# A two-layer hybrid block kernel: residual in a DRAM buffer during the mixers, shared half tiles, later decay tables, due dates for readers of PSUM

## The chip, the cores and the metric

The kernel runs on one core of a Trainium2 chip. The metric is the device time of one execution in microseconds (us). A core has a matrix engine (TensorE, in the profile PE, its weight loads PEld), a vector engine (VectorE, DVE), a scalar engine (ScalarE, ACT), GpSimd (POOL), and SyncE (SP), which here only issues DMA transfers. All of them work on an on-chip memory of 128 partitions (SBUF). TensorE writes to a smaller memory of eight banks (PSUM), which VectorE and ScalarE read.

## The reference

Two layers, 256 latent tokens and 256 context tokens, width 1024, all in fp32. Cut to what matters, for one stream:

```python
for l in range(DEPTH):
    mod = silu(c) @ w_mod[l] + b_mod[l]                  # 6 vectors of 1024: shift, scale, gate, twice
    h = rms_norm(x, norm_gain[l, 0]) * (1 + mod[1]) + mod[0]
    p = split_cols(h @ w_in[l])                          # q, k, v of four mixers, gate logits
    a, b, c_, d = gqa(p), retention(p), mla(p), diff_attention(p)
    y = sum(sigmoid(gate_n) * (mixer_n @ w_branch[l, n]) for n in range(4)) @ w_out[l]
    x = x + mod[2] * y
    h2 = rms_norm(x, norm_gain[l, 1]) * (1 + mod[4]) + mod[3]
    g, u = split(h2 @ w_ffn_in[l])
    x = x + mod[5] * ((silu(g) * u) @ w_ffn_out[l])      # hidden width 2816
```

The context goes through the same weights. Its queries are worked out in layer 0 only, since the second layer's context output is not needed.

## The kernel before

**Arithmetic.** Every fp32 matrix product is three products of a faster type: an operand is split into a rounded part (hi) and the remainder (lo), and hi\*hi, hi\*lo and lo\*hi are added up in a PSUM bank. For a weight unit of 128 x 512 the rounded copy (`whi`) is made by ScalarE or VectorE (`cp`) and the remainder (`wlo`) by VectorE (`tt`). The weights come in 512 KB loads (`wraw`, `mraw`) on SP's queue.

**Order.** The program is not run in the order in which it is written. `Builder` writes all operations to a `Recorder`. `schedule` first goes through them from the end (`backward`) and so gets for each operation the latest time at which it may end. `forward` then plays the engines with a cost for each operation: an engine that is free takes, among the operations whose inputs are ready, the one with the earliest due time. The orders thus found are emitted, one fixed queue for each engine. An operation that has variants (`cp`: ScalarE or VectorE) goes to the engine that is free, if `worth` says that the other would not finish sooner; `MARGIN` is added for the engine that isn't the first choice. `behind(lag)` keeps an operation from going before the TensorE operation that stands `lag` places ahead of it in the program.

**Tiles.** Nearly all data live in tiles of 128 x 512 fp32 of one common pool (`u`), of which there are `NU`; weight tiles may hold `W_LIMIT` of them. An operation whose output tile finds no free place in the pool is passed over by the planner (`allowed`). A PSUM tile is one of the eight banks.

**Stages of a layer.** The normed input is made in `gen_d` from the residual `xT` (eight tiles, fixed before the change) as eight tiles `hh` and eight `hl`. The projections of the mixers (`fill_*`) and the work of the heads (`jobs_*`: scores, softmax, transposes, products with v) are interleaved; head results go to `o`, four tiles for each mixer. Retention (`fill_ret`, `jobs_ret`) comes last and needs the decay tables (`rel`). Some gate logits are made early (`gate_logits`, tiles `glog`). Then `merge` multiplies each mixer's `o`, split by `split_o`, with its branch weights and sums the gated products (`glog`, `sig`); `out_proj` is the output projection, and only there `residual` updates `xT`. `ffn_in` and `ffn_out` follow; the split hidden values (`fh`, `fl`) are 44 tiles. In layer 0 a tile holds 512 tokens, in layer 1 only the 256 latent ones, so that half of such a tile is empty. `mod_vector` works out the vectors of `mod` ahead of their use, as sums of products on VectorE (`macc`).

Of the kernel before, what the change touches and what calls it, by code (L numbers as in the profile page):

```python
# [11 lines left out]
F32 = mybir.dt.float32  # L12
# [13 lines left out]
GRID_W = 64  # L26
OFF_GATE = 4512

NU = 73
DMA_LAT = 2.5  # L30
LOOKAHEAD = 1
RAW_BUFS = 7
# [1 line left out]
WRAW_LIMIT = 4  # L34
MRAW_LIMIT = 4
SLACK = 1
MARGIN = {"vector": -0.3, "scalar": -0.1, "gpsimd": 0}
W_LIMIT = 34
MOD_LAG = 600
REL_LAG = 200  # L40
DECAY_LAG = 0

MODS = {(0, ("merge", 1, 1)): [(0, 2, 2, 0.36)], (0, ("merge", 2, 1)): [(0, 3, 2, 0.385)],
# [20 lines left out]
class Recorder:  # L64
# [221 lines left out]
    def forward(self, users, deps, prio):  # L286
# [27 lines left out]
        self.times = {}  # L314

        held = 0.0

        def begin(v):
            return max(now, held) if v[6] else now
# [30 lines left out]
        while len(order) < n:  # L350
            while wait and wait[0][0] <= now + 1e-9:
                _, i = heapq.heappop(wait)
                for v in ops[i][0]:
                    heapq.heappush(heaps[v[0]], (prio[i], i))
            while ends and ends[0][0] <= now + 1e-9:
                _, i = heapq.heappop(ends)
                done[i] = True
                for nm in ops[i][2]:
                    t = tiles[nm]
                    t[3] -= 1  # L360
                    if t[3] == 0:
                        for tag in t[0]:
                            live[tag] -= 1
                            prof[tag][low:t[2] + 1] -= 1
                while low < n and done[low]:
                    low += 1
            nxt = wait[0][0] if wait else 1e18
            if ends:
                nxt = min(nxt, ends[0][0])
            for e in self.ENGINES:  # L370
                h = heaps[e]
                while h and issued[h[0][1]]:
                    heapq.heappop(h)
                if not h:
                    continue
                if free[e] > now + 1e-9:
                    nxt = min(nxt, free[e])
                    continue
                skipped = []
                found = -1  # L380
                while h and len(skipped) < 200:
                    p, i = heapq.heappop(h)
                    if issued[i]:
                        continue
                    if allowed(i) and (len(ops[i][0]) == 1 or worth(e, i, p)):
                        found = i
                        break
                    skipped.append((p, i))
                for x in skipped:
                    heapq.heappush(h, x)  # L390
                if found < 0:
                    continue
                i = found
                issued[i] = True
                for nm in ops[i][2]:
                    t = tiles[nm]
                    if not t[4]:
                        t[4] = True
                        for tag in t[0]:
                            live[tag] += 1  # L400
                            if t[1] > low:
                                prof[tag][low:t[1]] += 1
                pick[i] = next(x for x, v in enumerate(ops[i][0]) if v[0] == e)
                v = ops[i][0][pick[i]]
                end = begin(v) + v[4]
                free[e] = end
                if v[6]:
                    held = end
                self.times[i] = now
                if e == "sync":  # L410
                    free[e] = max(end, now + 0.565)
                heapq.heappush(ends, (end + (DMA_LAT if e == "sync" else 0.0), i))
                order.append(i)
                for u in users[i]:
                    left[u] -= 1
                    w = ops[u][0][0][0]
                    lat = 0.0 if e == "tensor" == w else v[5] + self.EXTRA[w]
                    est[u] = max(est[u], end + lat)
                    if not left[u]:
                        heapq.heappush(wait, (est[u], u))  # L420
                nxt = min(nxt, free[e])
            if nxt >= 1e18:
                raise RuntimeError("schedule stuck")
            now = max(now, nxt)
# [90 lines left out]
class Builder:  # L515
    def __init__(self, ctx, tc, a, out):
        self.tc, self.nc, self.a, self.out = tc, Recorder(tc.nc), a, out
        self.pool = ctx.enter_context(tc.tile_pool(name="sb", bufs=1))
        self.psum = ctx.enter_context(tc.tile_pool(name="ps", bufs=1, space=bass.MemoryType.PSUM))
        self.w = Weights(self)  # L520


# [119 lines left out]
    def setup(self):  # L642
# [3 lines left out]
        self.featT = self.fixed([128, 160], "featT")  # L646
        self.sil = self.fixed([128, 256], "sil")
        self.modT = [self.fixed([128, 96], "modT%d" % l) for l in range(DEPTH)]
        self.xT = [self.fixed([128, 512], "xT%d" % d) for d in range(KD)]
        nc.scalar.dma_start(out=self.ident, in_=a["ident"])  # L650
        rows0 = self.u(name="rows0")
        rows1 = self.u(name="rows1")
# [140 lines left out]
    def gen_d(self, l, which, ds):  # L793

        nc = self.nc
        nd = len(ds)
        av = self.sm(2 * nd).rearrange("p (d s) -> p d s", s=2)
        s0, s1 = min(self.rb), max(self.rb) + 1
        g = self.featT[:, 96 + 16 * l + 8 * which + ds[0]:96 + 16 * l + 8 * which + ds[0] + nd]
        c1 = 3 * which + 1  # L800
        nc.vector.scalar_tensor_tensor(
            out=av[:, :, s0:s1], in0=self.modT[l][:, 16 * c1 + 2 * ds[0]:16 * c1 + 2 * ds[0] + 2 * nd].rearrange(
                "p (d s) -> p d s", s=2)[:, :, s0:s1], scalar=1.0,
            in1=g.rearrange("p (d o) -> p d o", o=1).to_broadcast([128, nd, s1 - s0]), op0=ALU.add, op1=ALU.mult)
        for i, d in enumerate(ds):
            if d == len(self.hh):
                self.hh.append(self.u(F32R, "hhi"))
                self.hl.append(self.u(F32R, "hlo"))
            hi, lo = self.hh[d], self.hl[d]
            t = self.u(name="xn")  # L810
            for s, rb in self.rb.items():
                c = slice(s * 256, s * 256 + 256)
                nc.vector.scalar_tensor_tensor(out=t[:, c], in0=self.xT[d][:, c], scalar=av[:, i, s:s + 1],
                                               in1=rb, op0=ALU.mult, op1=ALU.mult)
                bias = self.mod(l, 3 * which, s)[:, d:d + 1]
                nc.scalar.activation(out=hi[:, c], in_=t[:, c], func=AF.Identity, bias=bias)
            for s in self.rb:
                c = slice(s * 256, s * 256 + 256)
                bias = self.mod(l, 3 * which, s)[:, d:d + 1]
                nc.vector.scalar_tensor_tensor(out=lo[:, c], in0=t[:, c], scalar=bias, in1=hi[:, c].bitcast(F32),  # L820
                                               op0=ALU.add, op1=ALU.subtract)


    def proj_tok(self, n, pairs, lhs, nk, kper, evac, cols=None):
# [464 lines left out]
    def fill_ret(self, l, qp, B):  # L1289
        nc = self.nc  # L1290
        B.update({"q": {}, "k": {}, "v": [{}, {}], "g": [{}, {}]})
        H = (self.hh, self.hl)
        self.rel = (self.u(name="rel0"), self.u(name="rel1"), self.u(name="rel2"))
        for i, n in enumerate((512, 512, 128)):
            with nc.behind(REL_LAG):
                nc.sync.dma_start(out=self.rel[i][:, :n], in_=self.a["rel"][:, 512 * i:512 * i + n])
        yield from self.heads_chunk(H, qp, 4, self.tabs["ret"], None, B["q"], None, norm=False)
        yield from self.heads_chunk(H, (0, 1), 4, self.tabs["ret"], None, B["k"], None, norm=False)
        for j in range(2):
# [356 lines left out]
    def jobs_ret(self, B, o):  # L1656
# [2 lines left out]
        qp = B["qp"]  # L1659
        qt = [t for p in qp for t in (2 * p, 2 * p + 1)]  # L1660
        st = {}
        rel0, rel1, rel2 = self.rel


        def decay(h):
# [121 lines left out]
    def gate_logits(self, tok, keep):  # L1787

        ps = [self.ps_acc(), self.ps_acc()]
        yield from self.proj_feat(2, (self.hh, self.hl), KD, tok, ps)  # L1790
        for m in range(2):
            g = self.u(name="glog")
            self.cp(g[:, :tok], ps[m][:, :tok])
            keep.append(g)

    def split_o(self, n, tok):
        hi_l, lo_l = [], []
        for k in range(4):
            hi = self.u(F32R, "ohi")
            lo = self.u(F32R, "olo")  # L1800
            self.split(hi[:, :tok], lo[:, :tok], self.o[n][k][:, :tok])
            hi_l.append(hi)
            lo_l.append(lo)
        self.o[n] = (hi_l, lo_l)
# [95 lines left out]
    def out_proj(self, l, tok, mp):  # L1900
# [4 lines left out]
        def flush():  # L1905
            for d in self.pend:
                self.stats(d, tok)
            self.pend = []
        if mp == 3 and tok == 512:
            yield from self.last_pair(l, 2, self.yy, KD, flush)  # L1910
            return
# [20 lines left out]
    def ffn_in(self, l, tok, j):  # L1932
# [29 lines left out]
        yield from self.proj_feat(2, H, KD, tok, pu)  # L1962
        for m in range(2):
            self.tt(sg[m][:, :tok], pu[m][:, :tok], sg[m][:, :tok], ALU.mult)
            hi = self.u(F32R, "fhi")
            lo = self.u(F32R, "flo")
            self.split_half(hi[:, :tok], lo[:, :tok], sg[m][:, :tok])
            self.fh.append(hi)
            self.fl.append(lo)
# [102 lines left out]
    def plan(self, l):  # L2072
# [12 lines left out]
            self.step(lst, gen, cost)  # L2085

        def newo(n):
            self.o[n] = [self.u(name="o") for _ in range(4)]
            return self.o[n]

        def start():
# [173 lines left out]
```

## Time and profile before

| | us |
|---|---|
| median of 3 runs | 1778.12 |
| lowest, highest | 1776.82, 1778.41 |
| the profiled execution | 1776.79 |
| its span, first to last instruction | 1774.9 |
| TensorE busy | 1726.4 |
| VectorE busy | 1334.3 |
| ScalarE busy | 846.9 |

Busy times are shares of one span and lie beside each other. Matmuls overlap in TensorE's pipeline and their ends are modelled, so that a busy TensorE isn't one at its peak. All recorded operations have line 432, that of the recorder's emission; they are told apart by their tiles. A row names the output tile, an arrow, and the inputs.

### The profile page before, as it was taken

What the parts mean: (1) busy time and instruction counts of PE and PEld (TensorE: products, weight loads), DVE (VectorE), ACT (ScalarE), POOL (GpSimd) and SP (SyncE); (2) the same over time, 40 slices, a digit from 0 to 9 for tenths busy, and PEclk for the clock granted to TensorE, in tenths of its full rate; (3) what the DMA queues carried; (4) which work ended last, traced back from release to release, by engine and by line L of the source; (5) the groups of instructions that cost most, each with busy time, mean ns of one, the idle gap of its engine ahead of it and who ended that gap; (6) DMA issues with size and microseconds to landing.
All of it is one profiled execution on the core that took longest, in us unless ns stands there. A gap on an engine that the chain in (4) does not pass through costs nothing. (4 is left out here: it accounts for less than half of the span.)

```text
span 1774.9 us, 30925 instructions
## 1 busy us (share of the span) xinstructions
PE 1726.4 (97%) x11510; PEld 1564.5 (88%) x11510; DVE 1334.3 (75%) x3055; ACT 846.9 (48%) x2014; POOL 58.7 (3%) x89
## 2 busy tenths in 40 slices
PE   7999999999899999999999999998999899999999
PEld 5988999998687887878888789997999789999999
DVE  5899999888989678786436533989989796786563
ACT  4378665556423333532222322666655544564441
POOL 0010000001010000000000000000000100000000
PEclk9999999999999999999999999999999999999999
DMA  9413113334546465355226522342234576756451
GB/s 310 165 45 117 50 35 110 93 96 125 166 154 193 151 214 166 108 189 189 83 72 197 189 89 75 110 118 63 72 93 129 148 222 190 233 161 183 138 187 62
DMA packets 204345, 243.72 MB, mean 137 GB/s; under 512 B 9994, under 2 KB 183204, under 8 KB 204196
## 3 DMA queue, kind: packets, MB, share of 16 engines
q1 hardware_dynamic: 203840, 241.61, 44.4%
q8 instruction: 90, 1.47, 0.3%
q14 instruction: 59, 0.48, 0.1%
q10 hardware_dynamic: 356, 0.14, 0.0%
HBM read 224.15 MB, written 1.05 MB: 127 GB/s over the span
## 5 line engine op out<-in xcount | busy, mean ns | idle before, releaser
L432 ACT CAST whi<-wraw 128x512 fp32r<-128x512 f32 (+3 forms) x630 | 361.1, 605 | 353.6 <-PE ps_acc L432 160.3
L432 DVE TENSOR_TENSOR wlo<-wraw,whi 128x512 fp32r<-128x512 f32 (+4 forms) x674 | 436.4, 668 | 120.2 <-PE ps_acc L432 65.7
L432 PE MATMUL ps_acc<-hhi,wlo 128*128 128x256 f32 (+1 forms) x864 | 292.7, 339 | 8.9 <-DVE wlo L432 6.1
L432 PE MATMUL ps_acc<-hlo,whi 128*128 128x256 f32 (+1 forms) x864 | 289.7, 335 | 0.2
L432 PE MATMUL ps_acc<-hhi,whi 128*128 128x256 f32 (+1 forms) x864 | 289.4, 335 | 0.0
L432 PE MATMUL ps_acc<-whi,hhi 128*128 128x256 f32 (+2 forms) x896 | 262.5, 293 | 1.2 <-ACT x L432 0.9
L432 PE MATMUL ps_acc<-wlo,hhi 128*128 128x256 f32 (+2 forms) x896 | 254.5, 284 | 0.3 <-DVE wlo L432 0.3
L432 PE MATMUL ps_acc<-whi,hlo 128*128 128x256 f32 (+2 forms) x896 | 254.6, 284 | 0.0
L432 PEld LDWEIGHTS ps_acc<-hhi,wlo 128*128 128x128 f32 x864 | 164.6, 191 | 28.4 <-DVE wlo L432 7.7
L432 PEld LDWEIGHTS ps_acc<-hlo,whi 128*128 128x128 f32 x864 | 164.6, 190 | 17.3 <-DVE hlo L432 0.7
L432 PEld LDWEIGHTS ps_acc<-hhi,whi 128*128 128x128 f32 x864 | 164.7, 191 | 14.9
L432 PEld LDWEIGHTS ps_acc<-whi,hhi 128*128 128x128 f32 x896 | 171.2, 191 | 3.0 <-ACT x L432 1.3
L432 PEld LDWEIGHTS ps_acc<-wlo,hhi 128*128 128x128 f32 x896 | 171.4, 191 | 1.0 <-DVE wlo L432 0.5
L432 PEld LDWEIGHTS ps_acc<-whi,hlo 128*128 128x128 f32 x896 | 171.0, 191 | 0.0
L432 DVE SCALAR_TENSOR_TENSOR macc<-mraw,sil,macc 128x512 f32<-128x512 f32 x224 | 157.8, 752 | 15.7 <-DMA mraw<-in_w_mod_dram 13.4
L432 PE MATMUL ps_acc<-fhi,wlo 128*128 128x256 f32 (+1 forms) x396 | 127.5, 322 | 0.0
L432 PE MATMUL ps_acc<-flo,whi 128*128 128x256 f32 (+1 forms) x396 | 126.2, 319 | 0.0
L432 PE MATMUL ps_acc<-fhi,whi 128*128 128x256 f32 (+1 forms) x396 | 126.1, 319 | 0.0
L432 PE MATMUL ps_s<-hhi,wlo 128*128 128x512 f32 (+1 forms) x352 | 119.2, 339 | 1.3 <-ACT hhi L432 1.3
L432 PE MATMUL ps_s<-hlo,whi 128*128 128x512 f32 (+1 forms) x352 | 119.1, 338 | 0.5 <-DVE hlo L432 0.5
L432 PE MATMUL ps_s<-hhi,whi 128*128 128x512 f32 (+1 forms) x352 | 119.0, 338 | 0.0
L432 PE MATMUL ps_s<-ohi,wlo 128*128 128x512 f32 (+1 forms) x256 | 88.4, 345 | 6.7 <-DVE glog L432 6.6
(247 smaller groups left out, 3563.5 us busy)
## 6 DMA issues: line engine op xcount, KB each, us to landing
wraw<-in_w_in_dram SPq DMA_DIRECT2D x124, 512.0 KB, 4.6
mraw<-in_w_mod_dram SPq DMA_DIRECT2D x96, 512.0 KB, 4.8
wraw<-in_w_ffn_in_dram SPq DMA_DIRECT2D x88, 512.0 KB, 3.5
wraw<-in_w_ffn_out_dram SPq DMA_DIRECT2D x40, 512.0 KB, 4.6
wraw<-in_w_branch_dram SPq DMA_DIRECT2D x32, 512.0 KB, 3.6
wraw<-in_w_out_dram SPq DMA_DIRECT2D x16, 512.0 KB, 4.9
stb<-sthi SPq DMA_DIRECT2D x36, 128.0 KB, 2.3
std<-stlo SPq DMA_DIRECT2D x24, 128.0 KB, 2.3
```

The costliest lines, as they stand in the source:

```text
L432: getattr(getattr(self.nc, eng), m)(*a, **k)
```

## The change

- `xT` moves from fixed tiles into the pool, and the pool grows by the eight tiles that this frees (`NU` 73 to 81). After the normed input for the mixers is made, `store` writes `xT` to a DRAM buffer `away`; in layer 1 only the latent half. `fetch`, at the start of each `out_proj`, loads the two tiles that it updates into new tiles of the pool, at the earliest some 60 places ahead in the program (`FETCH_LAG`).
- In layer 1 two half-filled tiles become one: gate logits, the split of `o`, the split hidden values, and `o` itself.
- The decay tables are loaded when the head work of retention is written, at most 100 places ahead (`REL_LAG` 200 before), and not when its projections are.
- When an operation that reads or writes PSUM on another engine than TensorE becomes ready, its due time is set to at most 12 us (`DUE`) after that moment.
- `MARGIN` for VectorE goes from -0.3 to 0.3; `W_LIMIT` from 34 to 40.

```diff
--- before.py
+++ after.py
@@ -26,7 +26,7 @@
 GRID_W = 64
 OFF_GATE = 4512
 
-NU = 73
+NU = 81
 DMA_LAT = 2.5
 LOOKAHEAD = 1
 RAW_BUFS = 7
@@ -34,10 +34,12 @@
 WRAW_LIMIT = 4
 MRAW_LIMIT = 4
 SLACK = 1
-MARGIN = {"vector": -0.3, "scalar": -0.1, "gpsimd": 0}
-W_LIMIT = 34
+DUE = 12.0
+MARGIN = {"vector": 0.3, "scalar": -0.1, "gpsimd": 0}
+W_LIMIT = 40
 MOD_LAG = 600
-REL_LAG = 200
+REL_LAG = 100
+FETCH_LAG = 60
 DECAY_LAG = 0
 
 MODS = {(0, ("merge", 1, 1)): [(0, 2, 2, 0.36)], (0, ("merge", 2, 1)): [(0, 3, 2, 0.385)],
@@ -314,6 +316,9 @@
         self.times = {}
 
         held = 0.0
+        prio = list(prio)
+        horizon = -min(prio)
+        reader = [o[0][0][0] != "tensor" and any(x.startswith("ps_") for x in o[2]) for o in ops]
 
         def begin(v):
             return max(now, held) if v[6] else now
@@ -350,6 +355,8 @@
         while len(order) < n:
             while wait and wait[0][0] <= now + 1e-9:
                 _, i = heapq.heappop(wait)
+                if reader[i]:
+                    prio[i] = min(prio[i], est[i] - horizon + DUE)
                 for v in ops[i][0]:
                     heapq.heappush(heaps[v[0]], (prio[i], i))
             while ends and ends[0][0] <= now + 1e-9:
@@ -517,6 +524,7 @@
         self.tc, self.nc, self.a, self.out = tc, Recorder(tc.nc), a, out
         self.pool = ctx.enter_context(tc.tile_pool(name="sb", bufs=1))
         self.psum = ctx.enter_context(tc.tile_pool(name="ps", bufs=1, space=bass.MemoryType.PSUM))
+        self.dram = ctx.enter_context(tc.tile_pool(name="dr", bufs=1, space=bass.MemoryType.DRAM))
         self.w = Weights(self)
 
 
@@ -646,7 +654,8 @@
         self.featT = self.fixed([128, 160], "featT")
         self.sil = self.fixed([128, 256], "sil")
         self.modT = [self.fixed([128, 96], "modT%d" % l) for l in range(DEPTH)]
-        self.xT = [self.fixed([128, 512], "xT%d" % d) for d in range(KD)]
+        self.xT = [self.u(name="xT") for d in range(KD)]
+        self.away = [self.tile(self.dram, [128, 512], F32, "away%d" % d, "away%d" % d, 1) for d in range(KD)]
         nc.scalar.dma_start(out=self.ident, in_=a["ident"])
         rows0 = self.u(name="rows0")
         rows1 = self.u(name="rows1")
@@ -819,6 +828,23 @@
                 bias = self.mod(l, 3 * which, s)[:, d:d + 1]
                 nc.vector.scalar_tensor_tensor(out=lo[:, c], in0=t[:, c], scalar=bias, in1=hi[:, c].bitcast(F32),
                                                op0=ALU.add, op1=ALU.subtract)
+            if which == 0:
+                self.store(l, d)
+
+    def store(self, l, d):
+
+        lo, hi = 256 * min(self.rb), 256 * max(self.rb) + 256
+        if l == DEPTH - 1:
+            hi = min(hi, 256)
+        if lo < hi:
+            self.nc.sync.dma_start(out=self.away[d][:, lo:hi], in_=self.xT[d][:, lo:hi])
+
+    def fetch(self, tok, ds):
+
+        for d in ds:
+            self.xT[d] = self.u(name="xT")
+            with self.nc.behind(FETCH_LAG):
+                self.nc.sync.dma_start(out=self.xT[d][:, :tok], in_=self.away[d][:, :tok])
 
 
     def proj_tok(self, n, pairs, lhs, nk, kper, evac, cols=None):
@@ -1290,10 +1316,6 @@
         nc = self.nc
         B.update({"q": {}, "k": {}, "v": [{}, {}], "g": [{}, {}]})
         H = (self.hh, self.hl)
-        self.rel = (self.u(name="rel0"), self.u(name="rel1"), self.u(name="rel2"))
-        for i, n in enumerate((512, 512, 128)):
-            with nc.behind(REL_LAG):
-                nc.sync.dma_start(out=self.rel[i][:, :n], in_=self.a["rel"][:, 512 * i:512 * i + n])
         yield from self.heads_chunk(H, qp, 4, self.tabs["ret"], None, B["q"], None, norm=False)
         yield from self.heads_chunk(H, (0, 1), 4, self.tabs["ret"], None, B["k"], None, norm=False)
         for j in range(2):
@@ -1659,7 +1681,11 @@
         qp = B["qp"]
         qt = [t for p in qp for t in (2 * p, 2 * p + 1)]
         st = {}
-        rel0, rel1, rel2 = self.rel
+        rel = (self.u(name="rel0"), self.u(name="rel1"), self.u(name="rel2"))
+        for i, n in enumerate((512, 512, 128)):
+            with nc.behind(REL_LAG):
+                nc.sync.dma_start(out=rel[i][:, :n], in_=self.a["rel"][:, 512 * i:512 * i + n])
+        rel0, rel1, rel2 = rel
 
 
         def decay(h):
@@ -1788,16 +1814,23 @@
 
         ps = [self.ps_acc(), self.ps_acc()]
         yield from self.proj_feat(2, (self.hh, self.hl), KD, tok, ps)
+        g = self.u(name="glog")
         for m in range(2):
-            g = self.u(name="glog")
-            self.cp(g[:, :tok], ps[m][:, :tok])
-            keep.append(g)
+            if m and tok == 512:
+                g = self.u(name="glog")
+            gv = g[:, m * 256:m * 256 + 256] if tok == 256 else g
+            self.cp(gv, ps[m][:, :tok])
+            keep.append(gv)
+
+    def parts(self, tok, name):
+
+        hi = self.u(F32R, name + "hi")
+        return (hi[:, 0:256], hi[:, 256:512]) if tok == 256 else (hi, self.u(F32R, name + "lo"))
 
     def split_o(self, n, tok):
         hi_l, lo_l = [], []
         for k in range(4):
-            hi = self.u(F32R, "ohi")
-            lo = self.u(F32R, "olo")
+            hi, lo = self.parts(tok, "o")
             self.split(hi[:, :tok], lo[:, :tok], self.o[n][k][:, :tok])
             hi_l.append(hi)
             lo_l.append(lo)
@@ -1906,6 +1939,7 @@
             for d in self.pend:
                 self.stats(d, tok)
             self.pend = []
+        self.fetch(tok, (2 * mp, 2 * mp + 1))
         if mp == 3 and tok == 512:
             yield from self.last_pair(l, 2, self.yy, KD, flush)
             return
@@ -1962,8 +1996,7 @@
         yield from self.proj_feat(2, H, KD, tok, pu)
         for m in range(2):
             self.tt(sg[m][:, :tok], pu[m][:, :tok], sg[m][:, :tok], ALU.mult)
-            hi = self.u(F32R, "fhi")
-            lo = self.u(F32R, "flo")
+            hi, lo = self.parts(tok, "f")
             self.split_half(hi[:, :tok], lo[:, :tok], sg[m][:, :tok])
             self.fh.append(hi)
             self.fl.append(lo)
@@ -2085,7 +2118,10 @@
             self.step(lst, gen, cost)
 
         def newo(n):
-            self.o[n] = [self.u(name="o") for _ in range(4)]
+            if last:
+                self.o[n] = [t[:, c:c + 256] for t in [self.u(name="o") for _ in range(2)] for c in (0, 256)]
+            else:
+                self.o[n] = [self.u(name="o") for _ in range(4)]
             return self.o[n]
 
         def start():
```

## Rows read from the trace of the kernel before

**Rows 1.** The page's first part: busy time, share of the span, instructions.
```profile
PE 1726.4 (97%) x11510; PEld 1564.5 (88%) x11510; DVE 1334.3 (75%) x3055; ACT 846.9 (48%) x2014; POOL 58.7 (3%) x89
```

**Rows 2.** By stage: us; busy (count) of PE, PEld, DVE, ACT, POOL; PEclk, DMA share, GB/s.
```profile
0.00:70.00 70.00, 60.24 (x485) 48.57 (x486) 47.66 (x163) 34.51 (x80) 0.52 (x5) 1.00 0.90 301
...
70.00:425.00 355.00, 351.33 (x2693) 335.03 (x2692) 322.65 (x837) 228.75 (x597) 20.61 (x36) 1.00 0.28 80
...
425.00:450.00 25.00, 22.67 (x136) 19.59 (x135) 23.79 (x70) 17.21 (x48) 3.02 (x4) 1.00 0.23 63
...
475.00:500.00 25.00, 19.68 (x80) 15.78 (x79) 22.85 (x35) 5.46 (x9) 4.03 (x3) 0.86 0.49 149
...
500.00:725.00 225.00, 225.00 (x1037) 182.80 (x1036) 175.20 (x289) 71.91 (x136) 11.81 (x11) 1.00 0.57 180
...
1200.00:1230.00 30.00, 22.81 (x144) 18.85 (x143) 28.69 (x80) 18.72 (x45) 2.45 (x2) 0.94 0.07 19
...
1385.00:1450.00 65.00, 54.46 (x386) 51.21 (x385) 56.65 (x156) 31.55 (x76) 4.01 (x6) 0.92 0.61 183
...
1450.00:1570.00 120.00, 119.35 (x991) 118.11 (x991) 88.52 (x181) 64.43 (x145) 0.00 (x0) 1.00 0.71 217
```

**Rows 3.** The same view of two dense stretches and one without transfers.
```profile
800.00:850.00 50.00, 50.00 (x222) 41.41 (x221) 27.40 (x43) 13.27 (x23) 0.00 (x0) 1.00 0.54 176
...
1600.00:1650.00 50.00, 50.00 (x419) 50.00 (x418) 30.56 (x62) 23.88 (x51) 0.00 (x0) 1.00 0.59 180
...
70.00:80.00 10.00, 10.00 (x84) 10.00 (x83) 7.78 (x25) 2.39 (x6) 0.00 (x0) 1.00 0.00 1
```

**Rows 4.** Timeline at 479: start, us, engine, operation, xcount [idle before <-releaser].
```profile
478.85 5.39 DVE L432 SCALAR_TENSOR_TENSOR macc<-mraw,sil,macc 128x512 f32<-128x512 f32 x8
...
484.15 1.28 DVE L432 SCALAR_TENSOR_TENSOR glog<-glog,ps_s 128x512 f32<-128x512 f32 x2
...
484.89 0.79 PE L432 MATMUL ps_s<-ohi,wlo 128*128 128x512 f32 x1 [5.32 <-DVE glog L432]
```

**Rows 5.** Timeline at 1216, ScalarE, VectorE and TensorE.
```profile
1217.82 0.64 ACT L432 COPY pvl<-ps_v 64x256 f32<-64x256 f32 x2 [2.68 <-DVE mq L432]
...
1218.50 0.42 DVE L432 TENSOR_TENSOR o<-ps_v,pvl 64x256 f32<-64x256 f32 x1
...
1218.97 0.58 PE L432 MATMUL ps_v<-pthi,v 128*128 128x256 f32 x1 [2.68 <-DVE o L432]
```

**Rows 6.** Timeline from 1385, VectorE.
```profile
1385.20 0.43 DVE L432 CAST whi<-wraw 128x512 fp32r<-128x512 f32 x1 [0.66 <-PE ps_acc L432]
...
1386.52 0.69 DVE L432 TENSOR_TENSOR wlo<-wraw,whi 128x512 fp32r<-128x512 f32 x1 [0.89 <-PE ps_acc L432]
```

**Rows 7.** Waits of TensorE in 1385 to 1450: us in total, times, longest.
```profile
PE ps_acc L432 <- DVE wlo L432: 5.5, 3, 2.5
...
PE ps_v L432 <- DVE ptlo L432: 1.8, 4, 0.5
...
PE ps_v L432 <- DVE pthi L432: 1.2, 2, 0.6
```

**Rows 8.** Groups by line, whole span, copies: xcount | busy us, mean ns | idle before.
```profile
L432 DVE CAST pthi<-ps_t 128x512 fp32r<-128x512 f32 x33 | 22.5, 684 | 2.8 <-PE ps_t L432 2.6
...
L432 DVE CAST whi<-wraw 128x512 fp32r<-128x512 f32 (+2 forms) x44 | 16.9, 385 | 9.7 <-DMA wraw<-in_w_in_dram 6.2 <-PE ps_acc L432 3.5
...
L432 ACT CAST pthi<-ps_t 128x512 fp32r<-128x512 f32 x67 | 38.5, 586 | 17.2 <-PE ps_t L432 13.1 <-PE ps_v L432 3.1 <-DVE o L432 0.4
...
L432 ACT CAST whi<-wraw 128x512 fp32r<-128x512 f32 (+3 forms) x630 | 361.1, 605 | 353.6 <-PE ps_acc L432 160.3 <-PE ps_s L432 56.3 <-DMA wraw<-in_w_in_dram 43.2
```

**Rows 9.** Waits of SP's queue in the opening, 0 to 62.
```profile
SPq L432 <- PE ps_acc L432: 15.2, 9, 3.7
```

**Rows 10.** DMA issues: xcount, KB each, median us to landing.
```profile
rel<-in_rel_dram SPq DMA_DIRECT2D x4, 256.0 KB, 2.7
...
out_dram<-out SPq DMA_DIRECT2D x4, 256.0 KB, 2.5
```

## The prediction

> **What bounds the kernel now.** I read the page's first part first [rows 1]: TensorE is busy 1726.4 of 1774.9 us, VectorE 75%, ScalarE 48%. So TensorE is the bound nearly everywhere, its instructions are not changed by the diff, and all there is to win is the time in which it stands still or runs at the lower clock. Then the table by stage [rows 2] says where that is. TensorE is idle 9.8 us in the opening (0 to 70), 3.7 in the whole of 70 to 425, 2.3 in 425 to 450, 5.3 in 475 to 500, 7.2 in 1200 to 1230 and 10.5 in 1385 to 1450; 500 to 725 has none. Idle time is not all that is lost, because matmuls overlap in the pipeline and their ends are modelled. A dense stretch gives the pace [rows 3]: 222 matmuls in 50 us where they are 512 columns wide (0.225 us each), 419 where they are 256 wide (0.119 us each). By that pace the 80 wide ones of 475 to 500 need 18.0 us, so 7.0 are lost there; the 386 of 1385 to 1450 need 46 us, so up to 19 are lost; the 144 of 1200 to 1230 need 17.2, so up to 12.8 (some are 512 wide, so less). The clock column gives the part that is not idle: it falls to 0.86, 0.92 and 0.94 in just these stretches.
>
> Next, what TensorE waits for in them. At 479 it wants a PSUM bank that VectorE has not yet read: VectorE does eight modulation products (macc, 5.39 us) that nobody needs for long, and only then the gate product that frees the bank; TensorE stands 5.32 us [rows 4]. At 1216 it waits 2.68 us for a bank that VectorE's add (o) is to free; the add needs a copy by ScalarE, and that copy stood 2.68 us with its releaser given as VectorE's mq, which reads nothing that the copy needs: it waited for the SBUF buffer that mq gave back [rows 5]. From 1385 VectorE waits for TensorE before a weight copy and its remainder (0.66 and 0.89 us), [rows 6], while in this stretch TensorE waits 5.5 us for such remainders, wlo [rows 7]: each waits for the other, which is what a pool without a free tile would look like.
>
> **The change, part by part.** No matmul, copy or product is added or removed; the edits change which engine and in which order, plus 32 transfers.
>
> Due dates. A PSUM reader now comes at the latest 12 us (planner's time) behind its readiness in the ranking. At 479 the gate product would precede the eight macc products. Gain: between 0 and the 7.0 us lost there; I take 6, since the row shows nothing else late. The macc products are late by then by the gate products' 1.28 us; their consumer, the residual of the first output projection, lies behind all the merges, so that costs nothing; without that cover it would cost the same 1.28. Queued behind a promoted reader are weight remainders (0.69 us each), and TensorE waits for those: see the rivals. In 425 to 450 I take 1 of the 2.3 idle us.
>
> The pool. With the residual away, 81 tiles serve the mixers instead of 73. Counted from the code, a mixer phase holds 16 tiles of hh/hl, up to 8 gate logits and up to 16 of o: 40, so 33 were free for heads, probabilities and weights, and 41 will be in layer 0. In layer 1 the shared halves make it 28 held of 81: 53 free. The later decay tables give three more tiles while the retention projections run, and weights may hold 40 instead of 34 tiles. In 1385 to 1450 (layer 1, retention and first merges) the gain lies between 0 and 19 us; I take 12, because the waits for wlo and their late clock are the larger part and some chains of head work (rs, pthi, ptlo) have no filler but the merges. In 1200 to 1230 it lies between 0 and 12.8; VectorE is busy 28.7 of 30 us there [rows 2], so the pool alone cannot empty it: I take 6, the 2.68 of the buffer wait, the same again from copies that leave VectorE, and a little of the clock. The feed-forward of layer 1 saves 22 tiles, but 1450 to 1570 has 0.65 us of idle time and the later merges show a full pace, so nothing.
>
> The margin. A copy now goes to VectorE only where ScalarE would end 0.3 us later, instead of 0.3 us sooner or less. VectorE makes 33 of the pthi copies (22.5 us) and 44 whi copies (16.9 us) [rows 8]; with some smaller groups perhaps 60 us, of which I estimate two thirds move. From PSUM that is cheaper (586 ns against 684), from SBUF dearer (605 against 385). ScalarE has the room: 229 of 355 us in 70 to 425 [rows 2]. Its worth is inside the 6 us above; without VectorE's backlog it is worth nothing.
> The Trainium skill, VectorE: DVE Perf Modes, section on the TRN2 errata, speaks against a part of it: its cycle table gives a 512-column copy from SBUF as an estimate of 327 ns on VectorE and 613 on ScalarE, so 44 moved whi copies would cost ScalarE 12.6 us more in all. By the rows it is 44 x 0.22 = 9.7 us. Either lies beside TensorE, and the sum is the same by both.
>
> The transfers. Stores: eight of 256 KB in layer 0 and eight of 128 KB in layer 1; fetches the same: 6.3 MB on SP's queue, beside 243 MB. The stores of layer 0 can go from the opening on. There the DMA share is 0.90 at 301 GB/s, so 2.1 MB take 7 us if all of it is pushed between weight loads that TensorE awaits; but SP itself stands 15.2 us in that stretch waiting for TensorE to free load buffers, [rows 9], and 70 to 80 carries no transfer at all [rows 3]. So between 0 and 7 us lost, nearer to the idle queue: 1. The fetches go where the share is 0.57 (500 to 725) and 0.71 (1450 to 1570). No row shows a fetch; the nearest is a 256 KB table that lands in 2.7 us, and for a store the output's 2.5 us [rows 10]. A fetch is let go some 60 operations before its projection, longer than a landing takes, so 0; at worst one landing per layer, 5.4 us. Weight loads behind a fetch on SP wait with it if its buffer is not free; with o and the gates gone by then, it is. The six decay loads move past the retention's weight loads on the same queue; they have the last projections as cover, and late they cost again a landing of 2.7 us per layer. The other idle time, in the opening and at the seams from residual to norm to first matmul, lies in chains that no edit shortens: 0.
>
> **Sum.** 6 + 1 + 6 + 12 - 1 = 24 us of the profiled execution. That one took 1776.8 us (span 1774.9), 1.3 below the median of the three, so 1752.8 for it and about 1753 to 1754 for a median; I say 1753.
>
> **The rivals.**
> All of it: the lost time of the four stretches (7.0 + 2.3 + 12.8 + 19 = 41) was want of tiles and wrong order only. Then 1737. For it speaks the mutual waiting; against it VectorE's 28.7 of 30.
> Only the order: VectorE's load (323 of 355 us in 70 to 425, 28.7 of 30 in 1200 to 1230), not the pool, makes the late stalls, and they only move. Then 6 less 1, about 1772. For it: 75% over the whole, over 90% in mixers. Against: VectorE stands waiting in the very stretch from 1385.
> The opening pays: all 7 us of stores land between loads and only the stall at 479 is saved. 1778, no change.
> Slower: ScalarE becomes the late engine. Some 100 copies in the two mixer phases lose their second engine; each then stands behind one whi copy of 0.6 us, and a transposed probability is on TensorE's path, so 60 us if all are exposed. It decides over the 24 us once some 40 of them are; with 60 exposed, 36 less 24: about 1790. For it: TensorE's waits on ptlo and pthi in 1385 to 1450, 1.8 and 1.2 us [rows 7]. Against: ScalarE's 48%. By the skill's table the 44 whi copies are the part that would feed it.
>
> **How the numbers follow.** My forecast (1742 to 1765) has 0.62; all of it 0.12; only the order 0.13; the opening 0.05; slower 0.08. For a range of 8 in 10 I leave out the slow case, half of the opening's and the far ends: 1735 to 1773. A measurement of this kernel can tell a change of about 0.2% from none, 3.6 us. All of the first three lie below 1774.5: faster 0.87; same 0.05; slower 0.08.
>
> **What would show it.** Right: no TensorE wait of 5 us on a gate product near 480, and the clock of that stretch at 1.00; idle time of the retention end in layer 1 down from 10.5 to some 4; fewer VectorE copies of pthi and whi; a span shorter by what these two stretches lost. The stores would stand in the opening's gaps or in 70 to 80, each fetch landed well before its residual. Wrong: TensorE waiting for a DMA of away, a longer opening, long waits for pthi from ScalarE, or the same lost time in the mixers at other places, which would mean that the order and not the room was at fault.

## The result, and the profile after

| | before, us | after, us |
|---|---|---|
| median (4 runs each) | 1777.47 | 1737.64 |
| lowest, highest | 1776.22, 1778.41 | 1736.88, 1738.32 |
| span of the profiled execution | 1774.9 | 1736.4 |

The ratio is 0.9776, with a 95% interval of 0.9759 to 0.9793: 39.8 us less, where 24 were forecast. The time lies at the low end of the range and on the first rival, "all of it" (1737).

The page's first part of the kernel after, to be read beside [rows 1]:

```profile
PE 1708.6 (98%) x11510; PEld 1556.6 (90%) x11510; DVE 1305.9 (75%) x3001; ACT 859.1 (49%) x2060; POOL 71.1 (4%) x97
```

The number of matmuls is the same. TensorE's idle time went from 48.5 to 27.8 us; the rest of the gain was never idle in the page, as it lay in the lower clock and under modelled ends.

To compare the two orders, I cut both spans at the same pieces of work: the first branch product of the merges of layer 0 (the first matmul with ohi), the first of the output projection (yhi), the first gate of the feed-forward (fsig), the last product of layer 0 (fhi), and the first output projection of layer 1. By stage, the kernel before (columns as in [rows 2]):

```profile
0.00:451.30 451.30, 435.54 (x3316) 404.25 (x3317) 395.40 (x1072) 281.77 (x725) 24.14 (x45) 1.00 0.38 114
451.30:683.50 232.20, 226.88 (x1006) 183.62 (x1005) 184.87 (x308) 76.17 (x132) 13.80 (x12) 0.99 0.57 179
683.50:744.70 61.20, 59.74 (x348) 49.39 (x347) 49.84 (x111) 25.62 (x97) 2.04 (x2) 1.00 0.44 140
744.70:1112.50 367.80, 366.45 (x1783) 305.42 (x1783) 194.50 (x336) 112.26 (x243) 4.96 (x4) 1.00 0.42 132
1112.50:1549.90 437.40, 418.57 (x3255) 403.43 (x3254) 375.11 (x958) 250.66 (x587) 13.80 (x26) 0.98 0.47 139
1549.90:1774.90 225.00, 219.21 (x1812) 218.40 (x1810) 134.60 (x276) 100.44 (x231) 0.00 (x0) 0.99 0.47 146
```

The same stages of the kernel after:

```profile
0.00:449.80 449.80, 435.07 (x3316) 404.51 (x3317) 383.89 (x1042) 289.58 (x746) 28.03 (x49) 1.00 0.39 119
449.80:673.70 223.90, 223.90 (x1006) 182.22 (x1005) 186.42 (x311) 80.07 (x140) 18.00 (x13) 1.00 0.62 193
673.70:740.10 66.40, 59.67 (x349) 50.80 (x348) 53.59 (x121) 26.03 (x101) 3.14 (x3) 0.95 0.44 143
740.10:1106.20 366.10, 366.10 (x1783) 305.37 (x1783) 190.70 (x326) 110.93 (x238) 4.78 (x4) 1.00 0.43 136
1106.20:1513.30 407.10, 406.17 (x3256) 396.81 (x3255) 361.88 (x936) 255.46 (x608) 17.13 (x28) 1.00 0.50 150
1513.30:1736.40 223.10, 217.71 (x1812) 216.88 (x1810) 129.47 (x270) 97.03 (x230) 0.00 (x0) 1.00 0.47 148
```

The matmul counts agree to within one, so the lines answer to each other. The mixers of layer 0 (first line) gained 1.5 us, its merges 8.3, its feed-forward 1.7; the mixers and merges of layer 1 gained 30.3; the last stage 1.9. The third stage, from output projection to feed-forward in layer 0 (the seam), lost 5.2. The sum is the 38.5 us of the spans. In layer 1's mixers TensorE is now idle 0.9 us of 407, against 18.8 of 437.

Three narrower stretches of the kernel after, which answer to 475:500, 1200:1230 and 1385:1450 of [rows 2]. Each is cut where the same number of matmuls has gone since its stage began; the orders differ, so it is as much work and not matmul for matmul the same:

```profile
473.65:491.33 17.68, 17.68 (x79) 14.64 (x78) 17.68 (x29) 4.62 (x8) 0.00 (x0) 1.00 0.69 212
1192.80:1210.61 17.81, 17.81 (x144) 17.32 (x143) 17.69 (x43) 16.09 (x40) 2.19 (x2) 1.00 0.00 1
1367.94:1414.09 46.15, 46.10 (x386) 45.76 (x385) 41.16 (x129) 30.99 (x76) 2.05 (x6) 1.00 0.59 178
```

Each is full and at full clock, and they are 7.3, 12.2 and 18.8 us shorter than before. In the second, VectorE is busy 17.69 of 17.81 us, more tightly than before (28.69 of 30), and yet TensorE makes in 17.8 us the 144 matmuls for which it had taken 30.

Copies in the kernel after, by group, against [rows 8]:

```profile
L439 DVE CAST whi<-wraw 128x512 fp32r<-128x512 f32 (+2 forms) x43 | 18.2, 429 | 7.4 <-DMA wraw<-in_w_in_dram 6.5 <-PE ps_s L439 0.5 <-DMA wraw<-in_w_branch_dram 0.3
...
L439 DVE CAST pthi<-ps_t 128x512 fp32r<-128x512 f32 x7 | 4.8, 685 | 0.0
...
L439 ACT CAST pthi<-ps_t 128x512 fp32r<-128x512 f32 x93 | 52.8, 591 | 15.7 <-PE ps_t L439 13.1 <-DVE sm L439 0.9 <-DVE t L439 0.8
```

VectorE's pthi copies fell from 33 to 7; its whi copies did not leave (44 to 43). The transfers, against [rows 10]:

```profile
away<-xT SPq DMA_DIRECT2D x8, 256.0 KB, 6.8
xT<-away SPq DMA_DIRECT2D x8, 256.0 KB, 4.3
...
away<-xT SPq DMA_DIRECT2D x8, 128.0 KB, 1.7
xT<-away SPq DMA_DIRECT2D x8, 128.0 KB, 2.2
```

TensorE waits for none of them: no wait in its list names away or a fetched tile. The fetches of layer 0 were issued from 664 to 692, ahead of their residuals.

### The profile page after: what moved, and what is told of

The parts are those of the page before. It is cut to its first block, busy times and chain, and to the rows that moved or that the text cites. A ratio compares the mean times of both kernels' runs of the same rounds, so it can differ in the third digit from the quotient of the medians.

```text
span 1736.4 us, 30865 instructions
## 1 busy us (share of the span) xinstructions
PE 1708.6 (98%) x11510; PEld 1556.6 (90%) x11510; DVE 1305.9 (75%) x3001; ACT 859.1 (49%) x2060; POOL 71.1 (4%) x97
## 4 chain that ended last, share of the span: by engine, by line
PE 85%; DVE 6%; DMA 4%; ACT 4%; issue 1%; SPq 1%; DVEq 0%; ACTq 0%
PE ps_acc L439 56%; PE ps_s L439 22%; PE ps_t L439 4%; PE ps_v L439 3%; DMA wraw<-in_w_in_dram 2%; DVE sm L439 2%; SPq L439 1%; ACT whi L439 1%; DMA stlo<-stlo 1%; DVE wlo L439 1%; ACT p L439 1%; DVE ptlo L439 1%; ACT pthi L439 1%; DVE xn L439 0%; DVE stlo L439 0%
## 5 line engine op out<-in xcount | busy, mean ns | idle before, releaser
L439 ACT CAST whi<-wraw 128x512 fp32r<-128x512 f32 (+2 forms) x631 | 358.5, 605 | 323.9 <-PE ps_acc L439 120.6
L439 PE MATMUL ps_acc<-fhi,whi 128*128 128x256 f32 (+1 forms) x572 | 139.8, 308 | 0.0
L439 PEld LDWEIGHTS ps_acc<-fhi,whi 128*128 128x128 f32 x572 | 96.6, 191 | 4.9
L439 PE MATMUL ps_s<-ohi,whi 128*128 128x256 f32 (+1 forms) x384 | 96.8, 318 | 0.0
```

The lines of the kernel that those rows point to most:

```text
L439: getattr(getattr(self.nc, eng), m)(*a, **k)
```

## The experiments

Two theories stood against each other. **Room**: the mixers lost time for want of free tiles. **Order**: they lost it because readers of PSUM stood behind work that could wait, and because VectorE was given too many copies. The table has the length of the stages of every kernel, cut at the same places as above (us of one profiled execution each, which lies up to 3.3 us off the median; median of 4 or 5 runs in the last column but one, ratio to the kernel before on the same chip in the last). The experiments ran on three chips, where the kernel before had medians of 1775.0, 1775.8 and 1778.7, so medians are compared to a few microseconds only, and the ratio is the surer column.

| kernel | mixers 0 | merges 0 | seam 0 | feed-forward 0 | mixers, merges 1 | rest | median | ratio (95%) |
|---|---|---|---|---|---|---|---|---|
| before | 451.3 | 232.2 | 61.2 | 367.8 | 437.4 | 225.0 | 1777.5 | 1 |
| after | 449.8 | 223.9 | 66.4 | 366.1 | 407.1 | 223.1 | 1737.6 | 0.9776 (0.9759 to 0.9793) |
| room alone | 449.7 | 231.9 | 61.1 | 370.7 | 422.2 | 222.7 | 1761.3 | 0.9919 (0.9905 to 0.9934) |
| order, old room | 447.3 | 228.3 | 65.0 | 366.2 | 427.3 | 222.6 | 1759.9 | 0.9915 (0.9900 to 0.9930) |
| no due dates | 448.8 | 235.1 | 61.1 | 368.5 | 425.7 | 222.7 | 1765.0 | 0.9942 (0.9927 to 0.9958) |
| due dates for gates only | 451.6 | 225.3 | 61.1 | 370.1 | 415.3 | 222.7 | 1745.6 | 0.9822 (0.9803 to 0.9840) |
| margin back | 449.3 | 224.3 | 68.0 | 367.5 | 412.6 | 223.1 | 1743.6 | 0.9818 (0.9801 to 0.9836) |
| residual stays in SBUF | 447.3 | 225.9 | 65.0 | 366.1 | 419.2 | 223.1 | 1748.9 | 0.9849 (0.9832 to 0.9865) |
| whole tiles | 446.5 | 223.9 | 66.8 | 366.1 | 418.7 | 223.1 | 1749.0 | 0.9850 (0.9836 to 0.9865) |
| decay tables early | 446.6 | 223.7 | 66.6 | 366.1 | 408.7 | 223.1 | 1734.9 | 0.9761 (0.9743 to 0.9779) |
| weight limit 34 | 448.6 | 223.7 | 66.1 | 366.2 | 409.0 | 223.8 | 1739.2 | 0.9785 (0.9765 to 0.9805) |
| due 13 us | 444.2 | 223.7 | 67.4 | 366.1 | 410.2 | 223.1 | 1736.3 | 0.9779 (0.9764 to 0.9793) |
| no due date for xn | 449.5 | 223.9 | 63.1 | 366.1 | 408.5 | 223.1 | 1734.4 | 0.9766 (0.9750 to 0.9782) |
| and none for mod | 447.6 | 223.9 | 62.9 | 366.1 | 408.7 | 223.1 | 1734.0 | 0.9754 (0.9737 to 0.9771) |

**How far the order alone scatters.** A due date of 13 us has no meaning of its own.

```diff
-DUE = 12.0
+DUE = 13.0
```

> The changed kernel with a due date of 13 instead of 12 us: a change with no meaning of its own, to see how far the planned order alone moves the time. If the gains are those of the mechanisms: 1737, within 3 us. If the 12 was a lucky order: 1745 or more.

1736.3, as forecast by the mechanisms. Its stages give the scale: 5.6 us in the mixers of layer 0 and 3.1 in those of layer 1, up and down. A difference of that size in one of these two stages says nothing in what follows.

**Room alone.**

```diff
-DUE = 12.0
-MARGIN = {"vector": 0.3, "scalar": -0.1, "gpsimd": 0}
+DUE = 1e9
+MARGIN = {"vector": -0.3, "scalar": -0.1, "gpsimd": 0}
```

> The changed kernel without due dates (DUE so large that it never applies) and with VectorE's margin back at -0.3: the room alone (residual in DRAM, 81 tiles, shared halves, later decay tables, weight limit 40). Theory of the room: the 30 us that the stretch from the end of layer 0 to the first output projection of layer 1 lost were want of free tiles, so most of them are gone here too; the stall of 7 us at the first merges of layer 0 comes back, and the seam of layer 0, which the changed kernel made 5 us longer, is as before: about 1740. Theory of the order: room without order is worth little, since VectorE is over 90% busy in the mixers: 1765 to 1775.

1761.3: between the theories. Room gives layer 1's mixers and merges 15.2 of the 30.3 us, and the merges of layer 0 nothing. What TensorE still waits for in that stretch of layer 1 (1113 to 1536):

```profile
PE ps_acc L439 <- DVE glog L439: 4.2, 1, 4.2
PE ps_s L439 <- ACT sig L439: 1.7, 1, 1.7
PE ps_acc L439 <- DVE ptlo L439: 0.9, 2, 0.6
```

The first two are gate products and gate activations. The waits for wlo of [rows 7], 5.5 us, are gone.

**Order in the old room.** The residual is in fixed tiles again (as in the diff of "The residual stays in SBUF"), the halves are whole tiles (as in "Whole tiles"), and:

```diff
-NU = 81
-W_LIMIT = 40
+NU = 73
+W_LIMIT = 34
```

> The changed kernel with the old room: residual in fixed tiles, 73 tiles, whole tiles for the halves, weight limit 34; due dates, margin and the later decay tables stay. Theory of the room: the stall of 7 us in the merges of layer 0 is gone, the seam of layer 0 is 5 us longer, and the mixers of layer 1 keep most of their lost time (some 25 of 30 us): about 1770. Theory of the order: the mixers of layer 1 are nearly as full as in the changed kernel: 1740 to 1748.

1759.9, again between. Order gives layer 1 10.1 us and the merges of layer 0 3.9. The two alone make 25.3 us in layer 1, and together 30.3; in the merges of layer 0 they make 4.2 and together 8.3. So each is worth more beside the other, though in layer 1 the 5 us between are not far above the scatter. By equal counts of matmuls the places differ. The stretch that answers to 1200:1230 takes 19.1 us with room alone and 19.0 with order alone, against 30.0 before and 17.8 with both: either closes it nearly whole, though the order in the old room loses 7.5 us ahead of it. The one that answers to 1385:1450 takes 53.2 and 57.7, against 64.9 and 46.1, and needs both.

**No due dates, all else as after.**

```diff
-DUE = 12.0
+DUE = 1e9
```

> The changed kernel without due dates, all else as it is. If due dates are worth the one stall in the merges of layer 0 and cost the seam of layer 0: 7 us come back and 5 go, about 1740, with TensorE's wait for a gate product (glog) of some 5 us near 475 and no waits for hlo of 2 us near 728. If they also keep the PSUM banks free in the mixers: the stretch of layer 1's mixers is 10 us or more longer, 1750 or above.

1765.0, so the second expectation held: due dates are worth 27 us beside the new room and the new margin (25.5 by the spans, 29 by the ratios), 18.6 of them in layer 1 and 11.2 in the merges of layer 0, less the 5 of the seam. With the old margin they are worth less, 18 us (room alone 1761.3, and 1743.6 in the run "The margin back"). The stall of [rows 4] came back and was longer. The timeline of this kernel at 478, VectorE and TensorE:

```profile
478.05 8.04 DVE L439 SCALAR_TENSOR_TENSOR macc<-mraw,sil,macc 128x512 f32<-128x512 f32 x12
486.00 1.88 DVE L439 SCALAR_TENSOR_TENSOR glog<-glog,ps_s 128x512 f32<-128x512 f32 x3
486.74 0.80 PE L439 MATMUL ps_s<-ohi,wlo 128*128 128x512 f32 x1 [9.60 <-DVE glog L439]
```

Twelve modulation products before the gate product, where there had been eight. The same kernel in layer 1:

```profile
1429.02 1.29 DVE L439 TENSOR_TENSOR wlo<-wraw,whi 128x512 fp32r<-128x512 f32 x2
...
1430.56 1.29 DVE L439 TENSOR_TENSOR wlo<-wraw,whi 128x512 fp32r<-128x512 f32 x2
1431.76 0.41 DVE L439 SCALAR_TENSOR_TENSOR glog<-glog,ps_s 128x256 f32<-128x256 f32 x1
...
1432.23 0.58 PE L439 MATMUL ps_acc<-hhi,wlo 128*128 128x256 f32 x1 [4.58 <-DVE glog L439]
```

With room to spare, VectorE makes weight remainders while TensorE stands, because the gate product that would free its bank is ranked behind them. At these two places the room is spent on the wrong work. The new margin, too, gains nothing without due dates: this kernel is no faster than room alone with the old one (1761.3).

**Due dates for the gates alone.**

```diff
-        reader = [o[0][0][0] != "tensor" and any(x.startswith("ps_") for x in o[2]) for o in ops]
+        reader = [o[0][0][0] != "tensor" and any(x.startswith("ps_") for x in o[2])
+                  and any(x.startswith(("sig", "glog")) for x in o[2]) for o in ops]
```

> The changed kernel with due dates for the gates alone: only operations that read PSUM and touch a gate tile (glog, sig) have one. If the 27 us that due dates are worth beside the new room are all gate products and gate activations that stand behind weight remainders and modulation products: as fast as the changed kernel or better, since xn at the seam has no due date here, 1732 to 1737, and the seam of layer 0 is back at 61 us. If readers in the heads' work (maxima, exponentials, copies of transposes) need due dates too: layer 1's mixers and merges lie some 5 to 10 us above 407, in all 1740 or more.

1745.6: the second expectation. The gates give 19 us of the net 27: all but 1.4 us in the merges of layer 0 and 10.4 of the 18.6 us in layer 1. Of the other 8 in layer 1, 7.3 lie in the stretch that answers to 1200:1230, heads' work with projections between: it takes 25.1 us, and 17.8 in the kernel after. TensorE waits there 2.7 us in one piece for ptlo, which reads a transpose from PSUM. Whether it is the readers of the heads or those of the projections that need their due dates, no run took apart. The seam is at 61.1.

**The margin back.**

```diff
-MARGIN = {"vector": 0.3, "scalar": -0.1, "gpsimd": 0}
+MARGIN = {"vector": -0.3, "scalar": -0.1, "gpsimd": 0}
```

> The changed kernel with VectorE's margin at -0.3 as before. If the copies that left VectorE matter: layer 1's mixers get 3 to 10 us longer, 1741 to 1748, and VectorE makes again some 80 us of copies. If VectorE's load is no limit once PSUM readers go first: 1737, within 3 us.

1743.6: 6 us by the medians, and 5.5 of the profiled execution's 8.4 are in layer 1, within the first expectation. VectorE is busy 372.8 us in that stretch, against 361.9.

**The residual stays in SBUF.** 73 tiles, no transfer.

```diff
-        self.xT = [self.u(name="xT") for d in range(KD)]
-        self.away = [...]
+        self.xT = [self.fixed([128, 512], "xT%d" % d) for d in range(KD)]
...
-            if which == 0:
-                self.store(l, d)
...
-        self.fetch(tok, (2 * mp, 2 * mp + 1))
```

> The changed kernel with the residual in its eight fixed tiles, 73 tiles in the pool, no store and no fetch; shared halves, weight limit 40, due dates and margin stay. If the eight tiles matter in both layers: the merges of layer 0 are back at 228 us, as with the whole old room (224 in the changed kernel), and layer 1's mixers and merges lie between 407 and 427: about 1748. If the shared halves alone give layer 1 room enough: only the 4 us of layer 0, 1741, less up to 2 for the opening without stores.

1748.9. The number came out as the first expectation had it, but not all its places: layer 1 is 12.1 us longer, and the merges of layer 0 only 2.0, not 4. The mixers of layer 0 have 447.3 without a store and 446.5 in the next kernel, which has all eight: the stores in the opening cost nothing that can be told from the scatter.

**Whole tiles.**

```diff
-        return (hi[:, 0:256], hi[:, 256:512]) if tok == 256 else (hi, self.u(F32R, name + "lo"))
+        return hi, self.u(F32R, name + "lo")
...
-                self.o[n] = [t[:, c:c + 256] for t in [self.u(name="o") for _ in range(2)] for c in (0, 256)]
+                self.o[n] = [self.u(name="o") for _ in range(4)]
```

(and a tile of its own for each gate logit.)

> The changed kernel without the shared halves (gate logits, split of o, hidden values and o in whole tiles in layer 1 too); the residual stays in DRAM, 81 tiles. If the eight tiles are the room that counts: as the changed kernel, 1737 to 1740. If layer 1 needs the halves: its mixers and merges go from 407 towards 427 and the sum to about 1748; layer 0 is as in the changed kernel in both cases.

1749.0: layer 1 needs the halves, 11.6 us. Beside the two runs above this is a scale. With the prediction's count of tiles free in layer 1's mixers, and due dates and margin on: 33 free tiles (old room) 427.3 us, 41 (whole tiles) 418.7, 45 (residual in SBUF) 419.2, 53 (after) 407.1. More room is less time, except for the middle pair, which lie closer than the scatter.

**The decay tables early, and the weight limit.**

```diff
-REL_LAG = 100
+REL_LAG = 200
```

(with the load back in `fill_ret`), and in another kernel

```diff
-W_LIMIT = 40
+W_LIMIT = 34
```

> The changed kernel with the decay tables loaded as early as before (at the retention's projections, lag 200). Their three tiles are missing from the pool for some 90 us of each layer. If free tiles decide in layer 1: 1 to 4 us longer, as three of the some twenty tiles of new room were worth in the runs without the DRAM buffer or the halves (11 us each). If not: 1737 within 3 us.

> The changed kernel with the weight limit at 34 tiles. If weights split ahead use the new room: 2 to 6 us longer in layer 1's mixers. If the room is used by the heads' tiles: 1737 within 3 us; a shorter time would mean that remainders made too early hold up others on VectorE.

1734.9 and 1739.2: neither can be told from the changed kernel by its stages. The first speaks against a plain count of tiles: three tiles for part of a layer cost nothing that can be seen. But the 1 to 6 us expected here lie about the scatter of layer 1 (3.1), so a small effect of either is not excluded.

**The seam.** The timeline of VectorE in the kernel after, at the seam of layer 0, and what TensorE waits for:

```profile
727.01 3.22 DVE L439 SCALAR_TENSOR_TENSOR xn<-xT,sm,ps_t 128x256 f32<-128x256 f32 x8
730.15 1.67 DVE L439 SCALAR_TENSOR_TENSOR hlo<-xn,modT,hhi 128x256 fp32r<-128x256 f32 x4
...
730.68 0.58 PE L439 MATMUL ps_acc<-hlo,whi 128*128 128x256 f32 x1 [1.80 <-DVE hlo L439]
```

The same place in the kernel before:

```profile
735.24 1.26 DVE L432 SCALAR_TENSOR_TENSOR xn<-xT,sm,ps_t 128x256 f32<-128x256 f32 x3 [0.58 <-PE ps_t L432]
736.51 0.49 DVE L432 SCALAR_TENSOR_TENSOR hlo<-xn,modT,hhi 128x256 fp32r<-128x256 f32 x1
736.91 0.47 DVE L432 SCALAR_TENSOR_TENSOR xn<-xT,sm,ps_t 128x256 f32<-128x256 f32 x1
```

xn reads the reciprocal norms from PSUM and so has a due date; hlo reads none. After the change all eight xn go first, and the first matmul of the feed-forward that needs hlo waits for it. The next kernel takes the due date from xn alone:

```diff
-        reader = [o[0][0][0] != "tensor" and any(x.startswith("ps_") for x in o[2]) for o in ops]
+        reader = [o[0][0][0] != "tensor" and any(x.startswith("ps_") for x in o[2]) and i not in self.calm
+                  for i, o in enumerate(ops)]
```

(`calm` holds the operations that touch a bank made by `gen_r`.)

> The changed kernel, but operations that read the bank of the reciprocal norms (the products xn of the normed input at the seams) get no due date. Theory: at the seam of layer 0 the due date pulls all eight xn, which read that bank, ahead of the first remainder hlo, which reads no PSUM, and TensorE waits twice some 2 us for hlo; without it xn and hlo alternate as before the change: 4 to 5 us less, about 1733, no wait for hlo over 0.5 us. Rival: the seam is longer because a modulation vector is finished there, or by the fetched residual; then 1737 as the changed kernel.

1734.4. The waits for hlo are gone and the seam is 3.3 us shorter, not 4 to 5: the cause is shown for these 3.3. The remaining 2 us over the kernel before are TensorE's waits for modrows (1.1) and the hhi behind it (1.8). The last kernel takes the due dates from the modulation vectors' readers too (a flag set in `mod_vector`):

> As the run in which the products xn have no due date, and besides none for the modulation vectors' copies and sums (modrows, modT). Theory: the 2 us by which the seam of layer 0 is still longer than before the change are the rows of a modulation vector that are pulled into it (TensorE waits 1.1 us for modrows and 1.8 us for the hhi behind it): 2 to 3 us less than 1734.4, about 1732. Rival: the readers of these banks free them late then, and the merges pay it: 1734 to 1737.

1734.0; the seam has 62.9 us and the same two waits (1.1 and 1.6). So that theory fell: their own due dates did not pull the modulation rows into the seam. Where the gates alone have due dates the seam is at 61.1 and the wait for hhi at 0.3, so the rest comes with the due dates of other readers; which, is open. The kernel has the lowest ratio of all, 0.9754, but its interval overlaps the changed kernel's: of the 3.6 us between their medians, only the 3.3 of xn have a place in the profile.

## Why the prediction was right, and where it was off

**What bounds the kernel: right.** The gain lay in time lost by TensorE in the merges of layer 0 and in two stretches of layer 1, and these are full now. The pace of a dense stretch was the right measure: by it up to 38.8 us were lost at 475, 1200 and 1385, and 38.3 came back there (7.3, 12.2 and 18.8), where the idle column alone showed 23. The prediction had these as upper bounds and took 6, 6 and 12; that is nearly the whole of the difference between 24 and what was measured. The fourth stretch, 425 to 450, cannot be told from the scatter of its stage. That the total meets the first rival's 1737 so closely is partly luck: the seam's loss of 5.2 us happens to cancel small gains in the other stages.

**Due dates: right at 479, mis-sized as a term.** The matmuls of 475:500, 25.0 us before, take 17.7 in each kernel that has due dates, 25.3 with room alone and 29.1 in the run without due dates: that stall was a matter of order only, as predicted. The sum had 6 + 1 for due dates. Beside the new room and margin they are worth 27 us. The one long wait in the rows was read rightly, but the term stopped at the wait that was there. The prediction asked what a promoted reader delays (weight remainders, with a TensorE that waits for them) and not what an unpromoted one suffers once the pool lets weight remainders run ahead. The run without due dates shows that: TensorE stands 4.58 us for a gate product behind a row of wlo, and 9.60 behind twelve macc.

**The pool: right in kind, mis-sized.** 12 + 6 us were set down for room and margin in layer 1. Room alone gives 15.2, room and margin without due dates 11.7, all three 30.3. The step that failed is "VectorE is busy 28.7 of 30 us there, so the pool alone cannot empty it". With room alone the matmuls of that stretch take 19.1 us and not 30, VectorE being as loaded as ever:

```profile
1202.90:1222.00 19.10, 18.26 (x144) 17.19 (x143) 18.91 (x59) 10.68 (x25) 0.00 (x0) 1.00 0.21 56
```

The kernel before itself spoke against the step: just ahead of the stretch VectorE is nearly as busy, and TensorE is full and makes 226 matmuls.

```profile
1170.00:1200.00 30.00, 29.84 (x226) 28.12 (x225) 27.87 (x84) 22.96 (x54) 2.08 (x2) 1.00 0.60 168
```

So a loaded VectorE did not by itself hold TensorE up; that TensorE then had other work ready is the likely reason, and is not shown. Which reading of the 2.68 us in [rows 5] is right, a buffer or merely an order, no run took apart: room alone and order alone both close that stretch.

**The margin: right in size, but only beside due dates.** Within the 6 us given; it moved the copies from PSUM (26 of the 33 pthi) but not the whi copies, and VectorE is busy 28 us less where 40 were to move. What the Trainium skill, VectorE: DVE Perf Modes, section on the TRN2 errata, had against it did not come into play, as the whi copies that a move would make dearer did not move (VectorE made 43, and 44 before). Those of 512 columns took 447 ns each on VectorE and 623 on ScalarE in the kernel after; by the section's table the estimates are 327 and 613, so the trace agrees with it for ScalarE and not for VectorE. The prediction's 385 against 605 mixed widths: at 512 columns the kernel before has 420 and 620.

**The transfers: nearly right.** Stores and fetches cost nothing that can be seen, where 1 us was taken. The landings were mis-sized: 6.8 us for a store in the opening where 2.5 was the nearest row, 4.3 for a fetch of layer 0 where it was 2.7; no engine waited for them.

**The seams: wrong.** "Chains that no edit shortens: 0" overlooked that an edit could lengthen one. xn is a PSUM reader, and the due dates moved all eight ahead of hlo: 5.2 us, of which 3.3 are shown to be that.

**The rivals.** "All of it" had 0.12 and is what happened. "Only the order" falls with the run in the old room, 22 us slower than with the new one, and "the opening pays" with the mixers' 447.3 and 446.5 without and with stores. For the slow one there is nothing: ScalarE took the copies and its share went from 48 to 49%, and TensorE waits 0.2 us in all for a pthi of ScalarE.

## What to carry to other kernels

In a planned order, an operation that empties a shared buffer must be ranked by what waits for that buffer, not by when its own result is used: data dependences do not show the second kind of user. More room and such a rank belong together; either alone gave about 15 us here and both 40, by the ratios. Check which other operations the rank takes along: a long-lived bank with many readers gained nothing from it and cost 3.3 us.

## What the runs showed of the hardware

A 256 KB store to DRAM landed in 6.8 us (median of eight, most of them issued between 60 and 70 us, where the DMA share was 1.00 and 368 GB/s moved), and a 128 KB store in 1.7 us where the share was 0.25 to 0.38. A VectorE busy 17.69 of 17.81 us went with a TensorE busy all of them. The clock was 0.86 in the stretch of the 5.3 us stand before the change and is 1.00 at the same place after; at the lengthened seam it is 0.95.
